# Turning the gated products of a feed-forward network by transposing DMA transfers instead of TensorE

## The chip, the cores and the metric

The kernel runs on one core of a Trainium2 chip. The metric is the device time of one execution in microseconds (us). For the kernel before, three runs gave a median of 916.63 us (916.10 to 916.77). One further execution was recorded by the profiler; it took 917.14 us, of which the profile's span (first to last recorded instruction) is 915.2 us.

## The reference

The reference is an encoder trunk of two layers for one sequence of 256 tokens, 1024 features wide, in float32. A layer mixes tokens by gated linear attention and by grouped attention, then runs a feed-forward network (FFN), then a small gated embedding. The change touches the FFN alone:

```python
FFN_HIDDEN = -(-8 * D_MODEL // (3 * 256)) * 256        # 2816
...
    gate, up = jnp.split(rms_norm(h, g_ffn_pre) @ w_ffn_in, 2, axis=-1)
    h = h + rms_norm((jax.nn.silu(gate) * up) @ w_ffn_out, g_ffn_post)
```

The product `silu(gate) * up` (256 tokens by 2816) is called the gated product below.

## The kernel before, in words

**Numbers.** Every float32 operand of a matrix product is split into a high and a low part, both in the type fp32r: `split` (L131 to L133) casts the high part on ScalarE (ACT) and subtracts it from the source on VectorE (DVE) for the low part. A product then takes three matmul passes (high·high, low·high, high·low) into one PSUM accumulator (`passes`, L113 to L121). TensorE (PE) contracts over partitions, so the left operand of each product has to stand with the contracted index on the partitions.

**Tiles.** Tokens come in two halves `hf` of 128. The 2816 hidden columns are 11 blocks of 256, so a block's gate and up together are 512 columns, one PSUM accumulator `acc`. Blocks 0 and 1 are computed by half: both for half 0, then both for half 1. Blocks 4, 5 and 10 (`PLAIN`) are computed for both halves at once (`block`). The other six blocks come as three pairs (`PAIRS`, beginning at 2, 6 and 8), each by seven products in place of eight in the manner of Strassen (`seven`). "o" steps (`out_step`) multiply finished gated products by `w_ffn_out`. The string `FFN` sets in which order block, pair and "o" steps are written in the program; the products of a block are consumed some 20 us or more after they are made, except those of the last pair.

**The turn.** A gated product comes out with tokens on the partitions (tile `sg`, from the pool `t512`, 128 by 512 float32), and `w_ffn_out` needs it with the hidden index on the partitions. Before the change PE turns it: `transpose_in` (L444 to L452, the transposes at L448) turns n squares of 128 by 128 into a PSUM tile `aux` by multiplying with the identity, and `hid.put` splits that tile into the FFN's `Split` object `hid`, whose tiles come from the pool `big` (ACT casts from PSUM, DVE subtracts from PSUM). `turned` (L1547 to L1552) does so with two squares for each half of blocks 0 and 1 and with four for each half of a pair; `block` has its own `turn` (L1582 to L1592, the transposes at L1587) with four squares for both halves together. In each layer that makes four turns of two squares, three of four squares for the plain blocks, and six of four for the pairs: 44 squares.

**What sets the order.** Each turn is a `Task`: a generator that yields a number of ticks before its next piece is written into the program. A tick comes twice per group of twelve matmuls of 512 columns (2.72 us), so one tick is about 1.36 us. `WAIT_FFN` 4, `WAIT_BLOCK` 6, `WAIT_PAIR` 9 and `WAIT_LAST` (3, 4) are these numbers. The framework's scheduler then makes the final order per engine from its own estimate of durations; `tc.high_priority(AHEAD)` lets the splits of a turn go ahead of other work. On the chip every engine runs its own list strictly in order.

**The weights.** All weights arrive by DMA transfers issued by SyncE (SP) at L296 (class `Stream`) into the pool `raw` (two buffers) or, for the pairs, into buffers lent from other pools (`lent`, `big`). ACT casts them into `wh` tiles and DVE subtracts for `wl` tiles (both L133, four buffers each, 128 by 1024 a half); a `raw` buffer is loaded again when DVE has finished with it. PE uses `wh` and then `wl` of each unit.

The pool `mid` holds tiles of 128 by 1024 float32 (512 KB); `halves` gives the two halves of one.

Of the kernel before, what the change touches and what calls it, by code (L numbers as in the profile page):

```python
# [10 lines left out]
F32 = mybir.dt.float32  # L11
F32R = mybir.dt.float32r
BF16 = mybir.dt.bfloat16
AF = mybir.ActivationFunctionType
ALU = mybir.AluOpType
AX = mybir.AxisListType

P = 128
T = 256
# [4 lines left out]

AHEAD, EMPTY, EMPTY_FIRST = 400, 100, 1600

WAIT, WAIT_FIRST, WAIT_FFN, WAIT_BLOCK = 6, 4, 4, 6

WAIT_NEXT, WAIT_IN, WAIT_H = (7, 9), ((6, 9), (6, 6)), ((3, 5), (3, 5))
WAIT_MIX = 3, 6  # L30
# [11 lines left out]
PLAIN, PAIRS = (4, 5, 10), (2, 6, 8)  # L42
OUT = (0, 1, 2, 3, 4, 5, 10, 6, 7, 8, 9)

WAIT_PAIR, WAIT_LAST = 9, (3, 4)


GATES = "uuu1u2m34m5m67m"
# [11 lines left out]
def trunk_kernel(ctx: ExitStack, tc: tile.TileContext, a: dict, out: bass.AP):  # L60
# [7 lines left out]
    nc = tc.nc  # L68
# [11 lines left out]
    part = ["start"]  # L80
# [8 lines left out]
    def mid(dt=F32):  # L89
        return b4p.tile([P, 1024], dt, tag="mid", name=nm("mid"))  # L90
# [34 lines left out]
    def vmul(out, in0, in1):  # L125
        nc.vector.tensor_tensor(out=out, in0=in0, in1=in1, op=ALU.mult)
# [4 lines left out]
    def split(hi, lo, src):  # L131

        return nc.scalar.copy(hi, src), nc.vector.tensor_tensor(out=lo, in0=src, in1=hi.bitcast(F32), op=ALU.subtract)  # L133
# [310 lines left out]
    def transpose_in(sp, src, k, n, hf, plain=None):  # L444

        ps = aux()
        for i in range(n):
            nc.tensor.transpose(ps[:, i * P : (i + 1) * P], src[:, i * P : (i + 1) * P], ident)  # L448
# [69 lines left out]
    def halves(t):  # L518
        return [t[:, j * 512 : (j + 1) * 512] for j in range(2)]
# [501 lines left out]
    for l in range(DEPTH):  # L1021
# [532 lines left out]
        for hf in range(2):  # L1554
            ws.lend = hf == 1
            for b in range(2):
                o = acc()
                for kh in range(2):
                    amode(o, u2, hf, kh * 4, us[b][kh], kh == 0, kh == 1, fresh=b == 0)
                sg = t512()  # L1560
                nc.scalar.activation(sg[:, 0:256], o[:, 0:256], AF.Silu)
                vmul(sg[:, 0:256], o[:, 256:512], sg[:, 0:256])
                turned(sg[:, 0:256], 2 * b, 2, hf)
                if hf == 1:
                    ws.done(2)
                if (hf, b) == (1, 0):
                    forms = sums(plain)

        def block(b):
            sg = t512()  # L1570
            o = [acc(), acc()]
            for kh in range(2):
                w = ws.take()
                for hf in range(2):
                    amode(o[hf], u2, hf, kh * 4, w, kh == 0, kh == 1)
                if kh == 1:
                    for hf in range(2):
                        c = slice(hf * 256, (hf + 1) * 256)
                        nc.scalar.activation(sg[:, c], o[hf][:, 0:256], AF.Silu)
                        vmul(sg[:, c], o[hf][:, 256:512], sg[:, c])  # L1580

                    def turn():  # L1582
                        yield WAIT_BLOCK
                        ps = aux()
                        for k in range(2):
                            for hf in range(2):
                                nc.tensor.transpose(  # L1587
                                    ps[:, k * T + hf * P : k * T + (hf + 1) * P],
                                    sg[:, hf * 256 + k * P : hf * 256 + (k + 1) * P], ident,
                                )  # L1590
# [3 lines left out]
                    t = Task(turn(), part[0], 2 * b // 4)  # L1594
                    for hf in range(2):
                        hid.makers[hf].append(t)
# [157 lines left out]
```

## Time and profile before

| | |
|---|---|
| median of three runs | 916.63 us |
| profiled execution | 917.14 us |
| span of its profile | 915.2 us |
| granted TensorE clock over the span | 0.999 of full |
| FFN of layer 0 (its turns) | about 266 to 424 us of the span |
| FFN of layer 1 | about 715 to 872 us of the span |

In a row of a profile a group's form `out<-in` names the tiles without their buffer numbers; `acc_0ffnin` is a PSUM accumulator of layer 0's FFN, `wh_0ffnin` and `wl_0ffnin` the parts of its weights. In timelines a row gives the start in us, the length in us, the engine, the line of the kernel, the operation and a count; a bracket at its end gives the idle time before it and who ended that. Rows of a matmul group overlap by a pipeline's depth, so the start of a row to the start of the next is what a group takes. A view of windows gives for each stretch its length and, per engine, the busy time and the count of instructions, then the granted clock, the DMA engines' busy share and GB/s.

### The profile page before, as it was taken

To read this page: it belongs to the slowest core of one execution; us is meant where nothing else is said; L and a number is where in the kernel's file an instruction comes from. 1 tells how busy PE (TensorE), PEld (TensorE's weight loads), DVE (VectorE), ACT (ScalarE), POOL (GpSimd) and SP (SyncE) were. 2 spreads that over 40 slices of the span, in tenths; PEclk is the share of its full clock that TensorE was granted. 3 is DMA by queue.
4 is the path that set the end of the run, shared out by engine and by line. 5 is a ranking of instruction groups with operands and counts; after the bars stand their busy time and mean duration, and the time that the engine had idled before them with its cause. 6 is when DMAs were issued, how large, how long until landed. Compare 5 with 4: busy or idle time off the path is not lost.

```text
span 915.2 us, 12243 instructions
## 1 busy us (share of the span) xinstructions
PE 905.9 (99%) x4551; PEld 769.6 (84%) x4551; DVE 791.1 (86%) x1025; ACT 584.5 (64%) x979; POOL 103.0 (11%) x157
## 2 busy tenths in 40 slices
PE   9999999999999999999999999999999999999996
PEld 8898888888878888888898888888888888888886
DVE  7899989987769998998779899799876898989984
ACT  6688777564567565566675687675644766565563
POOL 3700220400100000000334001110001000000001
PEclk9999999999999999999999999999999999999999
DMA  8664445657485655646576524455573856555361
GB/s 277 218 191 135 139 140 189 214 189 238 143 276 185 210 189 209 222 165 238 179 273 199 170 92 139 138 184 184 197 255 115 279 165 219 212 175 222 134 235 47
DMA packets 89512, 173.45 MB, mean 190 GB/s; under 512 B 3486, under 2 KB 27558, under 8 KB 88940
## 3 DMA queue, kind: packets, MB, share of 16 engines
q1 hardware_dynamic: 89292, 172.53, 55.7%
q8 instruction: 36, 0.59, 0.3%
q14 instruction: 24, 0.20, 0.1%
q10 hardware_dynamic: 160, 0.14, 0.0%
HBM read 169.50 MB, written 3.15 MB: 189 GB/s over the span
## 4 chain that ended last, share of the span: by engine, by line
PE 90%; DVE 4%; DMA 3%; issue 1%; ACT 1%; POOL 0%; SPq 0%; POOLq 0%; ACTq 0%; DVEq 0%
PE acc_1ffnin L121 12%; PE acc_0ffnin L121 10%; PE acc_1gate L121 7%; PE acc_0gate L121 7%; PE acc_1ffnin L105 7%; PE acc_0ffnin L105 4%; PE acc_1rq L121 3%; PE acc_1gqk L105 2%; PE acc_0gqk L105 2%; PE acc_1wout L121 2%; PE acc_0gg L121 2%; PE acc_1gg L121 2%; PE acc_1v L121 2%; PE acc_0v L121 2%; PE acc_1merge L121 2%; PE acc_0merge L121 2%
## 5 line engine op out<-in xcount | busy, mean ns | idle before, releaser
L133 ACT CAST wh_1ffnin<-raw_1ffnin 128x1024 fp32r<-128x1024 f32 x38 | 38.5, 1049 | 26.1 <-DMA raw_1ffnin<-in_w_ffn_out_dram 7.3
L133 ACT CAST wh_0ffnin<-raw_0ffnin 128x1024 fp32r<-128x1024 f32 x38 | 38.4, 1049 | 24.4 <-PE acc_0ffnin L121 7.8
L133 DVE TENSOR_TENSOR wl_1ffnin<-raw_1ffnin,wh_1ffnin 128x1024 fp32r<-128x1024 f32 x38 | 45.0, 1220 | 7.9 <-ACT wh_1ffnin L133 7.7
L133 DVE TENSOR_TENSOR wl_0ffnin<-raw_0ffnin,wh_0ffnin 128x1024 fp32r<-128x1024 f32 x38 | 44.9, 1220 | 7.7 <-ACT wh_0ffnin L133 7.6
L105 PE MATMUL acc_0ffnin<-wh_0ffnin,big_0ffnin 128*128 128x512 f32 x176 | 45.1, 390 | 0.0
L105 PE MATMUL acc_1ffnin<-wh_1ffnin,big_1ffnin 128*128 128x512 f32 x176 | 45.1, 390 | 0.0
L121 PE MATMUL acc_0ffnin<-wh_0ffnin,big_0wout 128*128 128x512 f32 x168 | 42.5, 393 | 0.0
L121 PE MATMUL acc_1ffnin<-wh_1ffnin,big_1wout 128*128 128x512 f32 x168 | 42.5, 393 | 0.0
L105 PEld LDWEIGHTS acc_0ffnin<-wh_0ffnin,big_0ffnin 128*128 128x128 f32 x176 | 33.0, 188 | 6.9
L105 PEld LDWEIGHTS acc_1ffnin<-wh_1ffnin,big_1ffnin 128*128 128x128 f32 x176 | 33.0, 188 | 6.9
L133 DVE TENSOR_TENSOR wl_1ffnin<-lent_1ffnin,wh_1ffnin 128x1024 fp32r<-128x1024 f32 x30 | 35.7, 1216 | 1.7 <-ACT wh_1ffnin L133 1.7
L133 DVE TENSOR_TENSOR wl_0ffnin<-lent_0ffnin,wh_0ffnin 128x1024 fp32r<-128x1024 f32 x30 | 35.7, 1216 | 1.7 <-ACT wh_0ffnin L133 1.7
L121 PEld LDWEIGHTS acc_0ffnin<-wh_0ffnin,big_0wout 128*128 128x128 f32 x168 | 31.1, 188 | 6.2
L121 PEld LDWEIGHTS acc_1ffnin<-wh_1ffnin,big_1wout 128*128 128x128 f32 x168 | 31.1, 188 | 6.2
L133 ACT CAST wh_0ffnin<-lent_0ffnin 128x1024 fp32r<-128x1024 f32 x30 | 30.7, 1053 | 7.1 <-PE acc_0ffnin L105 3.9
L133 ACT CAST wh_1ffnin<-lent_1ffnin 128x1024 fp32r<-128x1024 f32 x30 | 30.7, 1053 | 7.0 <-PE acc_1ffnin L105 3.9
L133 ACT CAST wh_0gate<-raw_0gate 128x1024 fp32r<-128x1024 f32 x20 | 20.0, 1048 | 17.0 <-DMA raw_0gate<-in_w_o_attn_dram 7.8
L133 DVE TENSOR_TENSOR wl_0gate<-raw_0gate,wh_0gate 128x1024 fp32r<-128x1024 f32 x20 | 24.0, 1247 | 7.5 <-ACT wh_0gate L133 7.4
L133 ACT CAST wh_1gate<-raw_1gate 128x1024 fp32r<-128x1024 f32 x20 | 19.9, 1048 | 14.0 <-DMA raw_1gate<-in_w_o_attn_dram 6.1
L133 DVE TENSOR_TENSOR wl_1gate<-raw_1gate,wh_1gate 128x1024 fp32r<-128x1024 f32 x20 | 23.5, 1218 | 5.3 <-ACT wh_1gate L133 5.2
L105 PE MATMUL acc_0ffnin<-wl_0ffnin,big_0ffnin 128*128 128x512 f32 x88 | 24.6, 394 | 0.0
L105 PE MATMUL acc_1ffnin<-wl_1ffnin,big_1ffnin 128*128 128x512 f32 x88 | 24.6, 394 | 0.0
(724 smaller groups left out, 2710.1 us busy)
## 6 DMA issues: line engine op xcount, KB each, us to landing
raw_0ffnin<-in_w_ffn_out_dram SPq DMA_DIRECT2D x11, 1024.0 KB, 5.2
raw_1ffnin<-in_w_ffn_out_dram SPq DMA_DIRECT2D x11, 1024.0 KB, 5.3
lent_0ffnin<-in_w_ffn_in_dram SPq DMA_DIRECT2D x6, 1024.0 KB, 7.3
lent_1ffnin<-in_w_ffn_in_dram SPq DMA_DIRECT2D x6, 1024.0 KB, 7.8
raw_0v<-in_w_in_dram SPq DMA_DIRECT2D x4, 1024.0 KB, 5.1
raw_0gate<-in_w_o_gla_dram SPq DMA_DIRECT2D x4, 1024.0 KB, 5.9
raw_0gate<-in_w_o_attn_dram SPq DMA_DIRECT2D x4, 1024.0 KB, 6.2
raw_0wout<-in_w_ffn_in_dram SPq DMA_DIRECT2D x8, 512.0 KB, 6.2
```

The lines of the kernel that those rows point to most:

```text
L105: return nc.tensor.matmul(o, lhsT, rhs, start=start, stop=stop)
L121: nc.tensor.matmul(o, x, y, start=start and n == 0, stop=stop and n == len(seq) - 1, **kw)
L133: return nc.scalar.copy(hi, src), nc.vector.tensor_tensor(out=lo, in0=src, in1=hi.bitcast(F32), op=ALU.subtract)
```

## The change

Nine of the eleven turns of a layer (all but the two of the last pair, beginning at block 8) no longer use PE. `turn_out` copies the gated product on ACT, read as 16-bit words, into one half of a `mid` tile, all low words of the float32 values first, then all high words ("planes"), and SP issues one DMA that transposes this half (128 by 1024 words, 256 KB, eight squares of 128 by 128) into the other half. Nine ticks later `take_in` joins the planes again on ACT, 16-bit words into float32 values, over the first half, and splits the result into `hid`, from SBUF now. Blocks 0 and 1 of a half share one tile and one turn of four squares, where before they had two turns of two. So a layer loses 36 transposes on PE and gains nine copies that take apart and nine that join, 128 by 1024 16-bit words each, on ACT, and nine transposing transfers on SP's queue; instead of four casts of 256 and nine of 512 columns from PSUM there are nine of 512 from SBUF and two from PSUM, and as many subtractions on DVE. Lines of the changed kernel are those of before plus one up to `transpose_in` and some 28 more behind it.

```diff
-WAIT, WAIT_FIRST, WAIT_FFN, WAIT_BLOCK = 6, 4, 4, 6
+WAIT, WAIT_FIRST = 6, 4
...
-WAIT_PAIR, WAIT_LAST = 9, (3, 4)
+WAIT_TURNED, WAIT_LAST = 9, (3, 4)
...
+    def turn_out(src, k, hf):
+
+        with tc.high_priority(AHEAD):
+            both, turned = halves(mid())
+            turned = turned.bitcast(U16)
+            parts = both.bitcast(U16).rearrange("p (s c) -> p s c", s=2)
+            words = src.bitcast(U16)
+            if hf is None:
+                nc.scalar.copy(
+                    parts.rearrange("p s (k h f) -> p s k h f", k=2, f=P),
+                    words.rearrange("p (h k f s) -> p s k h f", h=2, f=P, s=2),
+                )
+            else:
+                nc.scalar.copy(parts, words.rearrange("p (c s) -> p s c", s=2))
+            nc.sync.dma_start_transpose(out=turned.rearrange("p (x t) -> p x t", t=P), in_=parts.rearrange("p s c -> p (s c)"))
+        return both, turned
+
+    def take_in(sp, both, turned, k, hf):
+
+        n, tn = (2, T) if hf is None else (4, P)
+        hi, lo = sp.at(k, n, (hf or 0) * P, tn)
+        nc.scalar.copy(
+            both.bitcast(U16).rearrange("p (k t s) -> p k t s", s=2, t=tn),
+            turned.rearrange("p (s k t) -> p k t s", s=2, t=tn),
+        )
+        split(hi, lo, both.rearrange("p (k t) -> p k t", t=tn))
...
-        def turned(src, k, n, hf, wait=WAIT_FFN):
-
+        def turned(src, k, hf):

             def turn():
-                yield wait
-                transpose_in(hid, src, k, n, hf)
-
-            hid.makers[hf].append(Task(turn(), part[0], k // 4))
+                if k == 2 * PAIRS[-1]:
+                    yield WAIT_LAST[hf]
+                    transpose_in(hid, src, k, 4, hf)
+                else:
+                    x = turn_out(src, k, hf)
+                    yield WAIT_TURNED
+                    take_in(hid, *x, k, hf)
...
         for hf in range(2):
             ws.lend = hf == 1
+            first = t512()
             for b in range(2):
...
-                sg = t512()
-                nc.scalar.activation(sg[:, 0:256], o[:, 0:256], AF.Silu)
-                vmul(sg[:, 0:256], o[:, 256:512], sg[:, 0:256])
-                turned(sg[:, 0:256], 2 * b, 2, hf)
+                sg = first[:, b * 256 : (b + 1) * 256]
+                nc.scalar.activation(sg, o[:, 0:256], AF.Silu)
+                vmul(sg, o[:, 256:512], sg)
+                if b:
+                    turned(first, 0, hf)
...
-                    def turn():
-                        yield WAIT_BLOCK
-                        ps = aux()
-                        for k in range(2):
-                            for hf in range(2):
-                                nc.tensor.transpose(
-                                    ps[:, k * T + hf * P : k * T + (hf + 1) * P],
-                                    sg[:, hf * 256 + k * P : hf * 256 + (k + 1) * P], ident,
-                                )
-                        with tc.high_priority(AHEAD):
-                            hid.put(ps, 2 * b, 2, 0, T)
...
+                    turned(sg, 2 * b, None)
...
-                turned(sg, 2 * b, 4, hf, WAIT_LAST[hf] if b == PAIRS[-1] else WAIT_PAIR)
+                turned(sg, 2 * b, hf)
```

How this stands in the engines' lists (numbers behind the names are buffers' numbers). PE of the kernel before, at the first turn of a plain block (block 4, layer 0; `big_0wout` and `mid_0ffnin` are parts of the FFN's input):

```order
L121 MATMUL acc_0ffnin_2906<-wl_0ffnin_2854,big_0wout_2470 128x512 x4
L1587 MATMUL aux_0ffnin_2920<-ident,t_0ffnin_2783 128x128 x4
L121 MATMUL acc_0ffnin_2907<-wh_0ffnin_2853,big_0wout_2470 128x512 x8
L121 MATMUL acc_0ffnin_2907<-wl_0ffnin_2854,big_0wout_2470 128x512 x4
L121 MATMUL acc_0ffnin_2864<-wh_0ffnin_2878,mid_0ffnin_2747 128x512 x8
```

In the changed kernel the four transposes are gone, and so is every such group but those of the last pair; the matmul groups around them stand in the same order as before.

ACT of the kernel before, at the turns of blocks 0 and 1 of half 0, layer 0 (L1561 is the `Silu` of these blocks):

```order
L1561 ACTIVATE t_0ffnin_2669<-acc_0ffnin_2622 128x256
L133 CAST big_0ffnin_2666<-aux_0ffnin_2663 128x2x128
L1561 ACTIVATE t_0ffnin_2702<-acc_0ffnin_2672 128x256
L133 CAST big_0ffnin_2666<-aux_0ffnin_2697 128x2x128
L133 CAST wh_0ffnin_2711<-raw_0wout_2522 128x1024 x2
L133 CAST mid_0ffnin_2738<-mid_0wout_2297 128x512
```

The same place of the changed kernel (L468 takes apart, L476 joins):

```order
L1596 ACTIVATE t_0ffnin_2594<-acc_0ffnin_2622 128x256
L453 COPY mid_0wout_2298<-aux_0wout_2643 128x512
L468 COPY mid_0ffnin_2665<-t_0ffnin_2594 128x1024
L476 COPY mid_0ffnin_2665<-mid_0ffnin_2665 128x1024
L1596 ACTIVATE t_0ffnin_2668<-acc_0ffnin_2669 128x256
L134 CAST wh_0ffnin_2702<-raw_0wout_2522 128x1024 x2
L134 CAST mid_0ffnin_2729<-mid_0wout_2297 128x512
```

The first join stands directly behind the copy that feeds its transfer, so ACT waits there for the whole transfer, with a weight cast behind it. At the second turn two casts of 512 columns and a unit of weights stand between the two copies; in layer 1 the first turn's join stands nine rows further down, behind the second turn's take-apart.

SP's list at that place in the changed kernel; before, it held the same loads with none of the transposing transfers between them:

```order
L297 DMA raw_0emb_2589<-in_w_ffn_in_dram 128x4x256 x2
L469 DMA_TRANSPOSE mid_0ffnin_2665<-mid_0ffnin_2665 128x8x128
L297 DMA lent_0ffnin_2696<-in_w_ffn_in_dram 128x4x512
L297 DMA lent_0ffnin_2700<-in_w_ffn_in_dram 128x4x512
L297 DMA raw_0ffnin_2708<-in_w_ffn_in_dram 128x4x256 x2
L297 DMA raw_0ffnin_2761<-in_w_ffn_in_dram 128x4x256
L469 DMA_TRANSPOSE mid_0ffnin_2752<-mid_0ffnin_2752 128x8x128
L297 DMA raw_0ffnin_2761<-in_w_ffn_in_dram 128x4x256
L469 DMA_TRANSPOSE mid_0ffnin_2840<-mid_0ffnin_2840 128x8x128
```

Each transposing transfer waits on SP for its take-apart copy, with weight loads behind it; the load of `big_0ffnin` (one megabyte) that stood behind `raw_0emb` before now stands two units earlier.

More of the change, by code (lines that the diff above doesn't have):

```diff
@@ L13 @@
 BF16 = mybir.dt.bfloat16
+U16 = mybir.dt.uint16
 AF = mybir.ActivationFunctionType
@@ L1543, in trunk_kernel @@
         us = [[ws.take() for _ in range(2)] for _ in range(2)]
-        def turned(src, k, n, hf, wait=WAIT_FFN):
+        def turned(src, k, hf):
             def turn():
-                yield wait
-                transpose_in(hid, src, k, n, hf)
-            hid.makers[hf].append(Task(turn(), part[0], k // 4))
+                if k == 2 * PAIRS[-1]:
[5 more added lines that the diff above has]
+                    take_in(hid, *x, k, hf)
+            t = Task(turn(), part[0], k // 4)
+            for i in range(2) if hf is None else (hf,):
+                hid.makers[i].append(t)
         for hf in range(2):
             ws.lend = hf == 1
+            first = t512()
             for b in range(2):
@@ L1580, in block @@
                         vmul(sg[:, c], o[hf][:, 256:512], sg[:, c])
-                    def turn():
-                        yield WAIT_BLOCK
-                        ps = aux()
-                        for k in range(2):
-                            for hf in range(2):
-                                nc.tensor.transpose(
-                                    ps[:, k * T + hf * P : k * T + (hf + 1) * P],
-                                    sg[:, hf * 256 + k * P : hf * 256 + (k + 1) * P], ident,
-                                )
-                        with tc.high_priority(AHEAD):
-                            hid.put(ps, 2 * b, 2, 0, T)
-                    t = Task(turn(), part[0], 2 * b // 4)
-                    for hf in range(2):
-                        hid.makers[hf].append(t)
+                    turned(sg, 2 * b, None)
                 ws.done()
```

## The prediction

> **What bounds the kernel now.** I read the profile's totals and its chain first, then who waits for what on PE, then the stretches of the FFN. The totals and the first row of the chain:
>
> ```profile
> PE 905.9 (99%) x4551; PEld 769.6 (84%) x4551; DVE 791.1 (86%) x1025; ACT 584.5 (64%) x979; POOL 103.0 (11%) x157
> PE 90%; DVE 4%; DMA 3%; issue 1%; ACT 1%; POOL 0%; SPq 0%; POOLq 0%; ACTq 0%; DVEq 0%
> ```
>
> PE is busy 905.9 of 915.2 us and makes 90% of the chain. All that it waits for, over the whole span:
>
> ```profile
> PE warm L105 <- POOL seed L142: 1.0, 1, 1.0
> PE aux_1emb L994 <- DMA mid_0ffnout<-in_p_dram: 0.6, 1, 0.6
> PE acc_0rq L105 <- ACT wh_start L142: 0.5, 1, 0.5
> PE acc_0ffnin L121 <- ACT wh_0emb L133: 0.2, 1, 0.2
> ```
>
> Only the last wait, 0.2 us, lies in an FFN. So work taken off PE there is time won, until a weight tile comes too late. The view of windows: the two FFNs, then the densest 20 us of layer 0:
>
> ```profile
> 265.00:425.00 160.00, 160.00 (x727) 131.94 (x726) 146.88 (x145) 99.63 (x126) 0.95 (x1) 1.00 0.58 201
> 715.00:872.00 157.00, 157.00 (x717) 129.98 (x717) 143.63 (x143) 95.62 (x122) 0.00 (x0) 1.00 0.59 205
> 285.00:305.00 20.00, 20.00 (x92) 16.55 (x91) 20.00 (x19) 12.66 (x17) 0.00 (x0) 1.00 0.36 129
> ```
>
> PE has no gap. DVE (third pair of numbers) is busy 146.88 of 160 us and all of the 20; ACT (fourth) has 60 us free. The DMA engines are 0.58 busy.
>
> **The transposes that go.** The rows of the PSUM tile that they write:
>
> ```profile
> L448 PE MATMUL aux_0ffnin<-ident,t_0ffnin x32: 270/272/329, 266.8 to 421.7; 128*128 128x128 f32 x32
> L133 ACT CAST big_0ffnin<-aux_0ffnin x13: 360/579/588, 270.2 to 422.0; 128x512 fp32r<-128x512 f32 x9, 128x256 fp32r<-128x256 f32 x4
> L133 DVE TENSOR_TENSOR big_0ffnin<-aux_0ffnin,big_0ffnin x13: 414/680/692, 271.4 to 422.6; 128x512 fp32r<-128x512 f32 x9, 128x256 fp32r<-128x256 f32 x4
> L1587 PE MATMUL aux_0ffnin<-ident,t_0ffnin x12: 270/272/273, 297.9 to 340.9; 128*128 128x128 f32 x12
> ```
>
> Of 32 + 12 squares a layer, eight stay (the last pair): 36 go, in four bursts of two and seven of four. Their 272 ns overlap their neighbours, so I price a burst by the starts of rows in PE's timeline:
>
> ```profile
> 272.61 0.38 PE L448 MATMUL aux_0ffnin<-ident,t_0ffnin 128*128 128x128 f32 x2
> 272.75 2.08 PE L121 MATMUL acc_0ffnin<-wh_0wout,big_0wout 128*128 128x512 f32 x8
> 274.66 1.07 PE L121 MATMUL acc_0ffnin<-wl_0wout,big_0wout 128*128 128x512 f32 x4
> ...
> 297.88 0.60 PE L1587 MATMUL aux_0ffnin<-ident,t_0ffnin 128*128 128x128 f32 x4
> 298.24 2.08 PE L121 MATMUL acc_0ffnin<-wh_0ffnin,big_0wout 128*128 128x512 f32 x8
> 300.16 1.07 PE L121 MATMUL acc_0ffnin<-wl_0ffnin,big_0wout 128*128 128x512 f32 x4
> 301.07 1.98 PE L121 MATMUL acc_0ffnin<-wh_0ffnin,mid_0ffnin 128*128 128x512 f32 x8
> 302.88 1.07 PE L121 MATMUL acc_0ffnin<-wl_0ffnin,mid_0ffnin 128*128 128x512 f32 x4
> ```
>
> Eight matmuls alone take 302.88 − 301.07 = 1.81 us. With a burst of four ahead they take 300.16 − 297.88 = 2.28, so the burst costs 0.47; with two, 274.66 − 272.61 = 2.05, so 0.24. A layer gives back 7 × 0.47 + 4 × 0.24 = 4.25 us, both layers **8.5 us**. This is the whole gain; all else is cost, hidden or not.
>
> **Work added on ACT and DVE.** No 16-bit copy is in the trace. The nearest rows by count of elements, then by bytes:
>
> ```profile
> L133 ACT CAST wh_0ffnin<-raw_0ffnin 128x1024 fp32r<-128x1024 f32 x38 | 38.4, 1049 | 24.4 <-PE acc_0ffnin L121 7.8
> 275.24 1.67 ACT L133 CAST mid_0ffnin<-mid_0wout 128x512 fp32r<-128x512 f32 x3
> ```
>
> So a copy of 1024 words lies between about 0.55 us (as many bytes) and 2.1 us (twice the first row, if a stride of two words doubled it); I take 1.05, the row with as many elements. Eighteen copies a layer add 18.9 us to ACT's 99.6 of 160, less than its 60 us free; at 2.1 they would add 37.8, still less, but with no room in dense places. Casts and subtractions of the splits are a wash: on DVE 4 × 0.41 + 9 × 0.68 = 7.8 us before, 9 × 0.63 from SBUF (the rate of such subtractions in DVE's timeline) + 2 × 0.68 = 7.0 after. ACT also loses its waits for PE's transposes. None of this is on PE, so I cost it at nothing; the cover is the lead that weights have on PE, below.
>
> **The new wait.** ACT now waits at each join for a transfer, with weight casts queued behind it, DVE's subtractions waiting for those, and PE for both. Two numbers decide: T, from SP's issue to landing, and what ACT may be late.
>
> T is not in the trace. Rows of DMA issues (KB each, median us to landing):
>
> ```profile
> out_dram<-h SPq DMA_DIRECT2D x3, 256.0 KB, 2.0
> mid_0ffnout<-in_p_dram SPq DMA_DIRECT2D x1, 256.0 KB, 6.2
> lent_0ffnin<-in_w_ffn_in_dram SPq DMA_DIRECT2D x6, 1024.0 KB, 7.3
> mid_0ffnin<-in_g_ffn_post_dram SPq DMA_DIRECT2D x1, 512.0 KB, 8.3
> ```
>
> A plain transfer of the same 256 KB takes 2.0 us at the kernel's end with nothing ahead and 6.2 with traffic; 8.3 is the longest row. So T lies in 2.0 to 8.3, and above if turning is slower than copying. I take 4, midway between the two rows of the same size, since the DMA engines are 0.58 busy.
>
> Lateness is read from weights that follow a turn. The first turn of layer 0 is the worst: its join stands directly behind its take-apart. Rows of PE (what the product waits for, and the use of the weights behind it), ACT and DVE:
>
> ```profile
> 265.73 1.16 PE L121 MATMUL acc_0ffnin<-wl_0emb,big_0wout 128*128 128x512 f32 x4
> ...
> 273.34 2.01 ACT L133 CAST wh_0ffnin<-raw_0wout 128x1024 fp32r<-128x1024 f32 x2
> ...
> 274.50 2.35 DVE L133 TENSOR_TENSOR wl_0ffnin<-raw_0wout,wh_0ffnin 128x1024 fp32r<-128x1024 f32 x2
> ...
> 292.05 2.35 DVE L133 TENSOR_TENSOR wl_0ffnin<-raw_0ffnin,wh_0ffnin 128x1024 fp32r<-128x1024 f32 x2
> ...
> 280.37 1.08 PE L121 MATMUL acc_0ffnin<-wl_0ffnin,big_0wout 128*128 128x512 f32 x4
> ...
> 296.98 1.07 PE L121 MATMUL acc_0ffnin<-wl_0ffnin,big_0wout 128*128 128x512 f32 x4
> ```
>
> The product ends at 266.9; Silu 0.4, multiply 0.4 and take-apart 1.05 end at 268.8. The transfer lands at 268.8 + T, the join (1.05) and the next Silu (0.4) follow, and the weight cast that began at 273.34 begins at 270.2 + T: late by T − 3.1, 0.9 us at T = 4. Its low part was ready at 276.85 and used at 280.37, a lead of 3.5; but DVE then works without a gap to 305, and its tightest lead is at 294.4 against 296.98, 2.6 us. Four bursts less let PE come 1.0 earlier, which leaves 1.6. The first join therefore costs T − 4.7, nothing at 4.
>
> For the other joins the work between take-apart and join on ACT covers T: in layer 0 about 3.1, 3.3, 2.0, 6.6, 6, long, 4.6 and 3 us (of the order's rows at the durations above), in layer 1 the same but for the first (long) and second (4.2). With the next lead, 3.5, such a join costs T − gap − 3.5, nothing at T = 4. I allow **1 us** in all for meetings of several of them.
>
> **SP's queue.** Each transposing transfer waits on SP for ACT's take-apart, with weight loads behind it. SP waits anyway:
>
> ```profile
> SPq L296 <- DVE wl_0ffnin L133: 107.1, 21, 11.1
> ```
>
> 107 us in this FFN and its edges are spent waiting for DVE to free buffers, so a few tenths per issue vanish there; if an issue took several us, it would appear with T. The nine transfers of 256 KB move 2.4 MB a layer through engines 0.58 busy: hidden. One load of 1 MB now goes ahead of a unit that PE met 0.2 us late, and a store of 1 MB goes behind it. The first falls into idle DMA time; I cost the pair at 0, between −0.2 and +1.
>
> Sum against the profiled execution: 917.14 − 8.5 + 1 = 909.6; it ran 0.5 above the median of 916.63, so **909.1 us** on that scale.
>
> **A page against the change.** The Trainium skill, page "VectorE: DVE Perf Modes", section "The three transpose paths", lists 1309 ns for a 128×128 bf16 square by the DMA crossbar against 390 ns on TensorE, and its rules prefer TensorE where PSUM will do. If eight squares followed one another at that price, an estimate from that page gives T = 10.5, and the formulas for the stalls then give some 45 us, a time of about 953. The Trainium skill, "DMA: Bandwidth & Descriptors", section "Latency and other measured facts", gives transposing DMAs 261 GB/s, by which 256 KB move in 1.0 us, an estimate, and T stays near the short row. No row here shows either; PE's own square costs 0.12 us by the rows above.
>
> **Rivals.**
>
> Forecast, T up to 6: stalls of at most 1.3 for the first join and 0.5 each for the two with 2.0 us of cover, 2.3 in all. 908.1 to 911.5.
>
> Slower: **transposing is slow, so ACT stalls at its joins** with weights behind. Stalls by the formulas: at T = 7, 2.3 for the first, 2 × 1.5 where the cover is 2.0 us, 0.4 + 2 × 0.2 where it is 3.1 and 3.3, 2 × 0.5 where it is 3, together 7.1; at T = 7.2 they reach 8.5, where the change begins to lose; at T = 8.3, the longest row, 3.6 + 2 × 2.8 + 1.7 + 2 × 1.5 + 2 × 1.8 + 2 × 0.2 + 0.6 = 18.5, so 917.1 − 8.5 + 18.5 − 0.5 = 926.6, this rival's time. For it: nothing in the trace turns by DMA, the first join has no cover, DVE is at 92%. Against: the 2.0 us row. This is also the rival to which the page's price leads.
>
> No change: T near 7, or **DVE becomes the bound**: where it is busy 20 of 20 us, PE's pull-ahead finds weights late, and its 13.1 us of slack in this FFN shrink to 8.9 when the FFN is 4.25 shorter. For it: the lead of 2.6. Against: the gain by that place is 1.0, less than the lead. About 914.8 to 918.4.
>
> In between: ACT's copies cost 2.1 and eat part of the leads, 912 to 914.8.
>
> **How the numbers follow.** Forecast 0.45, in between 0.13, no change 0.08, slower 0.34. About 0.2% (1.8 us) is what a measurement of this kernel can tell from no change. Faster by more than that: 0.45 + 0.13 = 0.58; within it 0.08; slower 0.34. Faster's own range is 907.5 (no stall, the 0.2 gone, half a us of scatter) to 914.8. To leave out at most 2 in 10, the range must reach into the slow rival, over its time at the longest row: 907.5 to 930; what is left out is mostly T beyond 8.5.
>
> **What would show it.** Right: no row of PE with `ident` in the FFN but for the last pair; PE's busy time some 8 us less; the transfers landing in about 4 us; PE's waits still near 2 us. Wrong: PE waiting for `wl_0ffnin` or `wh_0ffnin` shortly behind a join, ACT's waits on the transposing transfer over 3 us each, ACT copies over 1.5 us, or DVE without a gap in the whole FFN. If the first turn of layer 0 stalls and that of layer 1 does not, T lies between 5 and 7.

## The result and the profile after

The changed kernel took 911.17 us (median of six runs, 909.68 to 911.95) beside 915.79 us for the kernel before (median of six in all). The ratio is 0.9947 with a 95% interval of 0.9934 to 0.9959: faster by 0.53%, 4.9 us. Run again later, beside experiments, it came to 0.9934 (0.9921 to 0.9948), 6.1 us. The profiled execution took 909.68 us, with a span of 907.9.

The totals and the chain, from the page of the kernel after:

```profile
PE 898.8 (99%) x4479; PEld 762.2 (84%) x4479; DVE 790.2 (87%) x1021; ACT 620.5 (68%) x1011; POOL 105.9 (12%) x157
PE 78%; DVE 11%; DMA 4%; issue 4%; ACT 2%; POOL 0%; SPq 0%; POOLq 0%; ACTq 0%; DVEq 0%
```

PE has 72 instructions and 7.1 us less, ACT 36 us more. PE's share of the chain fell from 90% to 78%, and DVE's rose from 4% to 11%: somewhere PE now runs at the pace of its weights. PE's waits over the whole span look harmless:

```profile
PE warm L106 <- POOL seed L143: 1.0, 1, 1.0
PE acc_0ffnin L106 <- DVE wl_0ffnin L134: 0.6, 2, 0.3
PE acc_0ffnin L122 <- DVE wl_0ffnin L134: 0.2, 1, 0.2
PE aux_0ffnout L449 <- DVE h L611: 0.2, 1, 0.2
```

All three waits for `wl` lie in layer 0, and PE waits 2.0 us in all. The windows of the two FFNs show the new load: ACT 115.51 and 116.82 us where it had 99.63 and 95.62, DVE about as busy as before (146.45 where it had 146.88, 146.66 where it had 143.63), and the DMA engines' share up from 0.58 and 0.59 to 0.70.

```profile
265.00:425.00 160.00, 159.10 (x699) 129.55 (x698) 146.45 (x143) 115.51 (x141) 1.41 (x3) 1.00 0.70 219
715.00:872.00 157.00, 157.00 (x698) 130.04 (x697) 146.66 (x145) 116.82 (x143) 0.86 (x2) 1.00 0.70 217
```

Where the time came from is best read off marks that both kernels have: the first matmul of each layer's FFN and one of the last. The view by tile gives first and last start of a group. Before:

```profile
L121 PE MATMUL acc_0ffnin<-wh_0wout,big_0wout x48: 389/389/478, 254.3 to 274.4; 128*128 128x512 f32 x48
L121 PE MATMUL acc_1ffnin<-wh_1wout,big_1wout x64: 387/389/481, 706.6 to 728.7; 128*128 128x512 f32 x64
L105 PE MATMUL acc_1ffnin<-wh_1ffnin,big_1ffnin x176: 387/389/481, 783.0 to 884.9; 128*128 128x512 f32 x176
```

After:

```profile
L122 PE MATMUL acc_0ffnin<-wh_0wout,big_0wout x48: 389/389/476, 253.7 to 273.1; 128*128 128x512 f32 x48
L122 PE MATMUL acc_1ffnin<-wh_1wout,big_1wout x64: 387/389/477, 703.6 to 725.3; 128*128 128x512 f32 x64
L106 PE MATMUL acc_1ffnin<-wh_1ffnin,big_1ffnin x176: 387/389/474, 778.2 to 877.7; 128*128 128x512 f32 x176
```

Layer 1's FFN went from 884.9 − 706.6 = 178.3 us to 877.7 − 703.6 = 174.1: **4.2 us won**, the 4.25 of the prediction. From the first mark of layer 0 to that of layer 1 the gain is (706.6 − 254.3) − (703.6 − 253.7) = **2.4 us**: 1.8 less. (The 0.6 us before the first mark is ahead of anything that the change touches. Layer 0's stretch also holds a wait of 0.6 us for `in_p` that the kernel before had, so it can win up to some 4.9.)

The loss sits where the prediction looked for it, behind the first join of layer 0. ACT's timeline there (the bracket is the idle time before a row and what ended it):

```profile
267.19 1.05 ACT L468 COPY mid_0ffnin<-t_0ffnin 128x1024 uint16<-128x1024 uint16 x1
274.00 1.17 ACT L476 COPY mid_0ffnin<-mid_0ffnin 128x1024 uint16<-128x1024 uint16 x1 [5.76 <-DMA mid_0ffnin<-mid_0ffnin]
275.07 0.38 ACT L1596 ACTIVATE t_0ffnin<-acc_0ffnin 128x256 f32<-128x256 f32 x1
275.35 1.99 ACT L134 CAST wh_0ffnin<-raw_0wout 128x1024 fp32r<-128x1024 f32 x2
```

ACT stands for 5.76 us, and the weight cast that began at 273.34 begins at 275.35, two us late by the clock and 2.6 by PE, whose first mark stands 0.6 us earlier: the prediction's T − 3.1 at T = 5.7. DVE hands the lateness on, since it works without a gap behind it, down to the unit that had the lead of 2.6 us:

```profile
293.92 2.35 DVE L134 TENSOR_TENSOR wl_0ffnin<-raw_0ffnin,wh_0ffnin 128x1024 fp32r<-128x1024 f32 x2
```

It ends at 296.27, and PE is there first:

```profile
293.33 2.30 PE L122 MATMUL acc_0ffnin<-wh_0ffnin,big_0wout 128*128 128x512 f32 x8
295.46 0.62 PE L122 MATMUL acc_0ffnin<-wl_0ffnin,big_0wout 128*128 128x512 f32 x2
296.33 0.74 PE L122 MATMUL acc_0ffnin<-wl_0ffnin,big_0wout 128*128 128x512 f32 x2 [0.24 <-DVE wl_0ffnin L134]
296.91 2.02 PE L122 MATMUL acc_0ffnin<-wh_0ffnin,big_0wout 128*128 128x512 f32 x8
...
341.39 0.63 PE L106 MATMUL acc_0ffnin<-wl_0ffnin,big_0ffnin 128*128 128x512 f32 x2
342.36 0.73 PE L106 MATMUL acc_0ffnin<-wl_0ffnin,big_0ffnin 128*128 128x512 f32 x2 [0.35 <-DVE wl_0ffnin L134]
342.93 2.00 PE L106 MATMUL acc_0ffnin<-wh_0ffnin,big_0ffnin 128*128 128x512 f32 x8
```

From start to start, the eight matmuls at 293.33 take 2.13 us instead of 1.81, and the four behind them 1.45 instead of 0.91: 0.9 us lost, of which the view of waits names 0.24. The rest of a stall is in longer steps between rows, so the marks are the better measure. The same happens at 341.39, 1.54 instead of 0.91, where three turns are packed into ACT's list: 0.6 more.

A stretch that holds both stalls and neither end of the FFN begins with the group at 274.66 in the kernel before (shown in the prediction) and ends with this one:

```profile
387.29 1.09 PE L121 MATMUL acc_0ffnin<-wl_0ffnin,big_0wout 128*128 128x512 f32 x4
```

The same two groups in the kernel after, and the third wait for `wl`, which lies outside:

```profile
273.38 1.07 PE L122 MATMUL acc_0ffnin<-wl_0wout,big_0wout 128*128 128x512 f32 x4
383.75 1.07 PE L122 MATMUL acc_0ffnin<-wl_0ffnin,big_0wout 128*128 128x512 f32 x4
420.48 0.73 PE L106 MATMUL acc_0ffnin<-wl_0ffnin,big_0ffnin 128*128 128x512 f32 x2 [0.25 <-DVE wl_0ffnin L134]
```

The stretch takes 112.63 us before and 110.37 after, 2.3 won; the experiments below show 3.8 where nothing is late, so some 1.6 are lost here. Around the third wait, at the end of layer 0's FFN, from the group that began at 420.43 before and 417.08 after to the turn of `h` (428.61 and 426.41), PE needs 9.33 us instead of 8.18, 1.15 more. The kernel without any turn, below, loses 0.6 there, so the transfers are at most a part of that cause; the rest is open. The wait for `in_p` that goes gives 0.8 back.

The tile that is turned shows what transfers and copies cost (min, median and max in ns, then first and last start):

```profile
L469 SPq DMA_TRANSPOSE mid_0ffnin<-mid_0ffnin x9: 1237/1250/1922, 268.3 to 377.1; - x9
L476 ACT COPY mid_0ffnin<-mid_0ffnin x9: 1168/1177/1183, 274.0 to 380.8; 128x1024 uint16<-128x1024 uint16 x9
L468 ACT COPY mid_0ffnin<-t_0ffnin x6: 1038/1044/1047, 267.2 to 376.0; 128x1024 uint16<-128x1024 uint16 x6
```

The copies take 1.04 and 1.18 us. The list of DMA issues gives a landing of 3.3 us in layer 0 and 3.6 in layer 1. These are not medians of nine: the profile tells the landing of one transfer in layer 0 and of three in layer 1.

```profile
mid_0ffnin<-mid_0ffnin SPq DMA_TRANSPOSE x9, 3.3
mid_1ffnin<-mid_1ffnin SPq DMA_TRANSPOSE x9, 3.6
```

The first of layer 0 is far off, issued at 268.3 and landed at 274.0: 5.7 us. ACT's waits at its joins tell of more: the second of layer 0, issued at 283.93, lets ACT go on at 290.24, 6.3 us later, of which ACT stands 3.4; the third and fourth take 3.2 and 3.6. The second does not hold DVE up: it works without a gap from 275.48 past 296.

### The profile page after: what moved, and what is told of

Read it like the earlier page. It is cut to its first block, busy times and chain, and to the rows that moved or that the text cites. A ratio compares the mean times of both kernels' runs of the same rounds, so it can differ in the third digit from the quotient of the medians.

```text
span 907.9 us, 12157 instructions
## 1 busy us (share of the span) xinstructions
PE 898.8 (99%) x4479; PEld 762.2 (84%) x4479; DVE 790.2 (87%) x1021; ACT 620.5 (68%) x1011; POOL 105.9 (12%) x157
## 4 chain that ended last, share of the span: by engine, by line
PE 78%; DVE 11%; DMA 4%; issue 4%; ACT 2%; POOL 0%; SPq 0%; POOLq 0%; ACTq 0%; DVEq 0%
PE acc_1ffnin L122 12%; PE acc_0gate L122 7%; PE acc_1gate L122 7%; PE acc_1ffnin L106 7%; DVE wl_0ffnin L134 6%; PE acc_1rq L122 3%; PE acc_0gqk L106 2%; PE acc_1gqk L106 2%; PE acc_1wout L122 2%; PE acc_0ple L122 2%; PE acc_1v L122 2%; PE acc_0gg L122 2%; PE acc_1gg L122 2%; PE acc_0v L122 2%; PE acc_0merge L122 2%
```

## The experiments

The theory after the result: all 8.5 us are there, and what is missing is lost in layer 0, because the first join has no cover and its transfer takes long. Rivals: ACT's added copies, the load of the transposing transfers on the DMA engines, and the packed stretch of ACT later in layer 0.

**No turn at all.** The split takes the product as it stands.

```diff
-                    x = turn_out(src, k, hf)
                     yield WAIT_TURNED
-                    take_in(hid, *x, k, hf)
+                    n, tn = (2, T) if hf is None else (4, P)
+                    split(*hid.at(k, n, (hf or 0) * P, tn), src.rearrange("p (k t) -> p k t", t=tn))
```

> Nine ticks after a gated product is done it is split as it stands, untransposed: no take-apart copy, no transfer, no join, so what w_ffn_out multiplies is left unturned. It keeps what the change removes (36 squares a layer on PE) and drops all that it adds. If PE's bursts are worth 8.5 us and nothing else limits the FFN (both theories), the time is 8 to 8.5 us under before: 0.9905 to 0.9915 of it. If the FFN of layer 0 is held by its weights even then (the rival that DVE or the weight loads are the bound), it gains only 5 to 7 us: 0.9925 to 0.9945.

Measured: 0.9915 (0.9901 to 0.9928), 7.8 us under before, at the edge of the 8 to 8.5 expected, and by the marks 4.1 us in layer 0 and 4.2 in layer 1, which is below called what a layer keeps. The PE term of the prediction holds within the interval. At the end of layer 0's FFN (before: 420.43 to 428.61) PE loses 0.6 us here too. This is about what any way of turning off PE can reach.

**Copies without transfers.**

```diff
-            parts = both.bitcast(U16).rearrange("p (s c) -> p s c", s=2)
+            parts = turned.rearrange("p (s c) -> p s c", s=2)
...
-            nc.sync.dma_start_transpose(out=turned.rearrange("p (x t) -> p x t", t=P), in_=parts.rearrange("p s c -> p (s c)"))
```

> The take-apart copy writes where the transfer would have written, and the join reads it there: both ACT copies stay, the transposing transfer is left out (so the squares are not turned). Theory of the wait (ACT stands at the joins until the transfer lands, and weights come late): nothing waits, so 7.5 to 8.5 us under before, like the kernel without any turn. Rival, ACT's 18 copies a layer themselves make weights late: stays at the changed kernel's 4.9 us under before, 0.994 to 0.996.

Measured: 0.9921 (0.9909 to 0.9933), 7.2 us under before, a little short of the 7.5 expected; layer 0 keeps 4.4 us. The copies are all but hidden: the rival that the copies alone keep the time at 4.9 us under before falls.

**A plain transfer in the transposing one's place.**

```diff
-            nc.sync.dma_start_transpose(out=turned.rearrange("p (x t) -> p x t", t=P), in_=parts.rearrange("p s c -> p (s c)"))
+            nc.sync.dma_start(turned, parts.rearrange("p s c -> p (s c)"))
```

> The same program order as the changed kernel, but each transfer of 256 KB copies its half tile plainly instead of transposing it (the squares are not turned). Theory of the wait: a plain transfer lands in 2.5 to 4 us in place of 3.3 to 6.2, ACT's first wait in layer 0 falls from 5.8 to under 4 us, and 7 to 8 us are gained against before. Rival that the place in the queue behind a megabyte of weights sets the wait, not the turning: the first wait stays above 5 us, and the gain near 5.

Measured: 0.9937 (0.9925 to 0.9949). The expectation of the theory failed in its first half. The first join of this kernel on ACT:

```profile
275.05 1.17 ACT L476 COPY mid_0ffnin<-mid_0ffnin 128x1024 uint16<-128x1024 uint16 x1 [6.69 <-DMA mid_0ffnin<-mid_0ffnin]
```

A plain copy of 256 KB at this place lands no sooner, 6.6 us after its issue at 268.4, and layer 0 keeps only 0.9 us while layer 1 keeps 4.2. So the rival came out: at this place the wait costs, whether the transfer turns or not. What sets the wait is taken up with the store below.

**Transfers that nobody waits for.**

```diff
-                    x = turn_out(src, k, hf)
+                    turn_out(src, k, hf)
                     yield WAIT_TURNED
-                    take_in(hid, *x, k, hf)
+                    n, tn = (2, T) if hf is None else (4, P)
+                    split(*hid.at(k, n, (hf or 0) * P, tn), src.rearrange("p (k t) -> p k t", t=tn))
```

> Take-apart copies and transposing transfers as in the changed kernel, but nothing reads what they bring: the split takes the unturned product, without a join. So the transfers' load on SP's queue and the DMA engines stays and ACT's wait and join go. Theory of the wait: 7.5 to 8.5 us under before. Rival, transposing transfers take the DMA engines from the weights (the engines' share in the FFN rose from 0.58 to 0.70): 4 to 6 us under before, with more waits of ACT on weights' transfers than without.

Measured: 0.9932 (0.9919 to 0.9945), between the two expectations. The marks decide more sharply than the time: layer 0 keeps 4.2 us and layer 1 4.2, although the DMA engines are as loaded as in the changed kernel:

```profile
265.00:425.00 160.00, 159.68 (x706) 130.93 (x705) 148.61 (x146) 107.39 (x134) 1.83 (x3) 1.00 0.72 221
```

In this profile the load alone delays PE's weights no more than in the kernel without any turn: PE waits 0.2 us for `wl` in both. The time leaves open up to 1.5 us for it, taken as the distance from the kernel without any turn, which is within the two intervals.

**The changed kernel again.** No edit.

> The changed kernel itself once more, for a second profile and more runs beside the others. Theory (layer 1 gives its whole 4.25 us, layer 0 loses about 2 of them at the first join and where its lateness shows later): 0.994 to 0.996 of before again, the stall in layer 0 again and none in layer 1.

Measured: 0.9934 (0.9921 to 0.9948). The stall was not there again in its profile:

```profile
272.98 1.17 ACT L476 COPY mid_0ffnin<-mid_0ffnin 128x1024 uint16<-128x1024 uint16 x1 [3.94 <-DMA mid_0ffnin<-mid_0ffnin]
```

Same program, same place: this time the first transfer landed 3.9 us after its issue (269.07), and layer 0 kept 3.9 us, layer 1 4.2. This execution took 908.60 us where the one with 5.7 us took 909.68. The others of this kernel lie between 909.09 and 911.95; what the first transfer took in them, no profile shows.

**The first join later.** It is held on ACT behind the last Silu of blocks 0 and 1.

```diff
+        silu = [None]
...
-                nc.scalar.activation(sg, o[:, 0:256], AF.Silu)
+                silu[0] = nc.scalar.activation(sg, o[:, 0:256], AF.Silu)
...
                     yield WAIT_TURNED
-                    take_in(hid, *x, k, hf)
+                    with tc.issue_after(silu[0].ins) if l == 0 and k == 0 and hf == 0 else nullcontext():
+                        take_in(hid, *x, k, hf)
```

> One join is moved: that of the first turn of layer 0 is held on ACT behind the Silu of block 1, half 1, which puts it behind the second turn's take-apart, as layer 1 has it. Transfers, copies and all else stay. Theory of the wait at this one join: ACT's wait of 5.8 us there goes, layer 0 keeps some 4 us, and the time falls by 1 to 2.5 us to 0.992 to 0.9935. Rival, the loss in layer 0 comes from the transfers' load or from ACT's packed stretch later (about 320 to 350 us): no change from the changed kernel, 0.9945 to 0.996.

Measured: 0.9927 (0.9915 to 0.9940). Layer 0 keeps 4.7 us, as the theory has it, but layer 1 only 2.9 in this profile, whose chain runs through two loads of weights there; why they were late is open. Its ratio is 0.0007 below that of the changed kernel on the same chip, its median 0.2 us above: the time does not tell them apart.

**The first turn back on PE.**

```diff
-                if k == 2 * PAIRS[-1]:
-                    yield WAIT_LAST[hf]
+                if k == 2 * PAIRS[-1] or l == k == hf == 0:
+                    yield WAIT_LAST[hf] if k else 4
                     transpose_in(hid, src, k, 4, hf)
```

> One turn is undone: the first of layer 0 (blocks 0 and 1, half 0) goes back to four transposes on PE after four ticks; the other 17 stay as changed. It gives back 0.47 us of PE. Theory of the first join: the stall that it caused, 1 to 2.5 us, goes, so 0.5 to 2 us faster than the changed kernel, 0.9925 to 0.9942. Rival (load, packed ACT): 0.2 to 0.5 us slower than the changed kernel.

Measured: 0.9919 (0.9907 to 0.9932), 908.41 us, 0.9 us under the changed kernel's median on the same chip though it pays one burst on PE. PE waits for no weights in its FFNs; layer 0 keeps 5.0 us, layer 1 only 3.3, its chain running through the same two loads. The direction is the theory's, the size within the scatter.

**Issued by ACT.**

```diff
-            nc.sync.dma_start_transpose(
+            nc.scalar.dma_start_transpose(
```

> The transposing transfers are issued by ACT behind its take-apart, on ACT's own DMA queue, not behind the weights' loads on SP's. If the first transfer takes 5.7 us because a megabyte of weights is ahead of it in SP's queue (the plain one took 6.6 there), it lands in 3 to 4 us here and layer 0's stall shrinks; against that, 18 issues of 1.25 us now stand on ACT, 11 us a layer: together within 1.5 us of the changed kernel either way. If the engines are simply shared between queues, the first transfer stays at 5 us or more and the time rises by 1 to 3 us.

Measured: 1.0454 (1.0435 to 1.0473), 41 us slower than before. Neither expectation came near. ACT at the first join, then ACT's waits at the joins of both layers, and what PE waits for most:

```profile
279.95 1.16 ACT L476 COPY mid_0ffnin<-mid_0ffnin 128x1024 uint16<-128x1024 uint16 x1 [10.79 <-DMA mid_0ffnin<-mid_0ffnin]
```

```profile
ACT mid_0ffnin L476 <- DMA mid_0ffnin<-mid_0ffnin: 34.4, 6, 10.8
ACT mid_1ffnin L476 <- DMA mid_1ffnin<-mid_1ffnin: 17.7, 6, 7.7
```

```profile
PE acc_0ffnin L122 <- ACT wh_0ffnin L134: 11.9, 4, 4.3
PE acc_1ffnin L122 <- ACT wh_1ffnin L134: 5.3, 3, 3.7
```

On a queue of its own the first transfer takes 10.7 us, and SP no longer holds the two loads of 1 MB behind it: they are issued at 269.07, it at 269.19. This is the prediction's slow rival in the flesh. By its formula the first join costs T − 4.7 = 6.0 us. The issues themselves, 18 of 1.25 us, add 22 us of work to ACT, so not all of the 41 are waits.

**The store behind the first transfer.** On SP, one store of 1 MB changes places. `turns` collects the issues of the transposing transfers.

```diff
         if l == 0:
-            kept = keep_embedding()
+            made = next(embedding)
+            kept = keptp.tile([P, 2, D], F32, tag="kept", name=nm("kept"))
...
+        if l == 0:
+            with tc.issue_after(turns[0].ins):
+                nc.sync.dma_start(kept, made)
```

> The changed kernel with one transfer moved on SP's queue: the store of 1 MB (the embedding kept for later) that was issued at about 260.5 us, eight us ahead of the first transposing transfer, now follows that transfer and two loads. ACT's order stays as in the changed kernel, the first join directly behind its take-apart. If the first transfer's 3.9 to 5.7 us come from the backlog of the DMA engines (busy all of 264 to 276 us), it now lands in 3 to 3.6 us, ACT's first wait falls under 3.5 us, layer 0 keeps 4 us and the time is 0.9915 to 0.993 of before. Rival, the time is the transposing itself or the loads behind it: 3.9 to 5.7 us as before and 0.9934 to 0.9947.

Measured: 0.9923 (0.9909 to 0.9938), 908.63 us. ACT at the first join:

```profile
271.84 1.17 ACT L478 COPY mid_0ffnin<-mid_0ffnin 128x1024 uint16<-128x1024 uint16 x1 [3.63 <-DMA mid_0ffnin<-mid_0ffnin]
```

The transfer lands 3.6 us after its issue (268.24), and layer 0 keeps 4.9 us, layer 1 4.2, with the join still directly behind its take-apart. That fits the backlog; but one of the changed kernel's own profiles had 3.9, and the interval overlaps with 0.9934, so this one profile alone would not settle the cause of T.

The DMA packets in the traces go further. The two loads of 512 KB issued 2.7 us ahead of the first transposing transfer move in packets of 1 KB, the store in packets of 8 KB, the transfer in packets of 256 bytes. In all six profiles in which SP issues that transfer, its last packet ends 0.91 us after the last packet of these two loads. The loads end 2.1 and 2.3 us after the transfer's issue in the two kernels with the store moved; where the store is ahead, 2.4 us in the profile with 3.9, and 3.9 to 4.9 in three others (4.1 in the one with 5.7). The store's own last packet lies 1.2 us before the issue in the profile with 3.9, and 0.3 to 0.7 in the three. So the first transfer waits for the loads ahead of it, and these are late where the store still ran among them. That is six profiles, not a time of many runs.

**Plain transfers issued by ACT.** `nc.scalar.dma_start(turned, ...)` in the transposing transfer's place.

> Plain transfers of the same 256 KB in place of the transposing ones (the squares are not turned), issued by ACT on its own queue, as in the kernel whose transposing transfers took 4.4 to 10.7 us there. If a second queue shares the engines packet by packet with the weights' loads, and the 256-byte packets of the transposing transfer lose by that, the plain one with its 2 KB packets lands in 3 to 6 us and the time is 0.99 to 1.00 of before. If any transfer on a second queue is late whatever its packets, it lands in 7 us or more and the time stays above 1.03.

Measured: 1.0174 (1.0147 to 1.0200), between the two expectations. The lists of DMA issues give the plain transfer's median landing, first on SP's queue (the kernel above), then on ACT's (this one):

```profile
mid_0ffnin<-mid_0ffnin SPq DMA_DIRECT2D x9, 256.0 KB, 4.3
mid_1ffnin<-mid_1ffnin SPq DMA_DIRECT2D x9, 256.0 KB, 3.0
```

```profile
mid_0ffnin<-mid_0ffnin ACTq DMA_DIRECT2D x9, 256.0 KB, 5.6
mid_1ffnin<-mid_1ffnin ACTq DMA_DIRECT2D x9, 256.0 KB, 4.4
```

So on the second queue the transfers land later, by 1.3 and 1.4 us, though these rows rest on few landings (one and three on SP's queue, one and five on ACT's), and the kernel is 22 us slower than with the plain transfer on SP's (18 issues of 0.47 us on ACT included); that it transposes costs 26 more (issues of 1.25 us included). How the engines share out their time between queues, these runs do not show.

**Store and first join both later.** The moves of the first join and of the store, together. The edit is the sum of the two above.

> All nine turns a layer by transposing transfers, the store moved behind the first of them, and the first join of layer 0 held behind the second turn's take-apart. With no wait left that outlasts its cover, it keeps what a kernel without any turn keeps, less the copies' part: 0.9915 to 0.9925 of before. If the later packed stretch of ACT in layer 0 or the joins of layer 1 still cost, 0.993 to 0.9945.

Measured: 0.9924 (0.9911 to 0.9937), 908.55 us; layer 0 keeps 4.6 us, layer 1 4.2. It adds nothing to the store's move alone. Three orders (0.9919, 0.9923, 0.9924) are below both measurements of the changed kernel by their medians and come within 0.8 us of the kernel without any turn; against the changed kernel of 0.9947 and 0.9934 the intervals overlap in part.

What a layer keeps carries a scatter: ahead of 274.66, where no more than one burst of 0.24 us is gone, the kernels already differ by 1.1 us. The stretch between two groups of layer 0 (274.66 to 387.29 in the kernel before) tells the kernels apart where the whole time does not. In us:

| kernel | loads ahead end, after the transfer's issue | ACT's wait at the first join | won in the stretch |
|---|---|---|---|
| changed, first profile | 4.1 | 5.8 | 2.3 |
| changed, again | 2.4 | 3.9 | 3.8 |
| plain transfer | 5.4 | 6.7 | 0.5 |
| traffic only | 3.9 | no join | 3.8 |
| first join later | 4.9 | 0 | 3.8 |
| store later | 2.1 | 3.6 | 3.8 |
| store and join later | 2.3 | 0 | 3.8 |
| first turn on PE | no transfer | no join | 3.8 |
| copies without transfers | no transfer | 0 | 3.7 |
| no turn at all | no transfer | no join | 3.8 |

With the first join later, the transfer is as late as ever and nothing is lost. So it is ACT's wait at this one join that costs. The packed stretch of ACT at 320 to 350 us stands in the kernels with 3.8 too; by itself it loses nothing, and costs only where DVE is already late.

## Why the prediction was right, and where its size was off

It forecast 909.1 us, 7.5 under the median it had, with a range to 930; measured were 4.9 and, again, 6.1 us. The mechanism, the sign and the place of the loss were right.

- **The transposes** (8.5 us): right. Layer 1 gave 4.2 or 4.3 in both profiles of the changed kernel and in six others. In layer 0 the stretch of the table gave 3.7 or 3.8 wherever the first wait was short or gone. At the FFN's end 0.6 to 1.0 us are lost in all of these but the kernel with the first turn on PE, the kernel without any turn included, and 0.8 is won at `in_p`.
- **ACT's copies** (1.05 us each, hidden): right. 1.04 and 1.18 us; the kernel with copies and no transfers is within 0.6 us of the one with neither.
- **DVE as the bound**: not by itself. It is busy 146.45 of 160 us in layer 0, as before, and PE passes with a wait of 0.2 to 0.3 us when ACT is on time, as it does without any turn. But once ACT is late, DVE has no gap in which to catch up.
- **T of 4 us**: the term that was mis-sized, at the first two joins of layer 0. Elsewhere 3.1 to 4.3 us can be read in the two profiles of the changed kernel, near the 4 taken, which was luck as much as reasoning: the two rows it stood between were of other places and other loads. The first transfer, with no cover, took 5.7 us in one profile and 3.9 in another, and 4.7 is where it begins to cost. The second took 6.3, which by the formula (T less a cover of 3.1 and a lead of 3.5) costs nothing. The formula T − 4.7 for the first gives 1.0 us at 5.7; PE lost 0.9 there, and nothing at 3.9. What I took from the midpoint of two rows should have been worked out from what SP had issued just before at this very place: 3 MB within the nine us ahead of it (SP's timeline: two loads of 512 KB at 259.4, the store at 260.4, two loads at 265.5).
- **The allowance of 1 us**: too small. Behind a late first join DVE stays late, and at ACT's packed stretch, 320 to 350 us, PE lost another 0.6; the prediction had no term for a lateness that comes back. In the first profile layer 0 loses 1.8 us net; in the medians 2.4 to 3.6 of the 8.5 are missing, by the two ratios, of which the kernel without any turn misses 0.7. The rest is not shown by any profile, since the profiled executions were the fastest of their runs.
- **The slow rival** (T over 7.2): not this kernel. Its sign, a wait of ACT over 3 us, did appear at two joins (5.8 and 3.4 us), and the sign for T between 5 and 7, a stall in layer 0 and none in layer 1, fits the first profile. Transfers on ACT's queue made the rival real, 41 us.
- **The load that moved ahead and the store that moved behind** (priced at 0): the load was harmless; PE's wait for the first weights, 0.2 us before, is gone in one profile of the changed kernel and 0.2 in the other. The store then stood eight us ahead of the first transposing transfer and still ran among the loads that this transfer waited for; behind it, the loads ended at 2.1 and 2.3 us, against 2.4 and 4.1 in the changed kernel's two profiles.

## What to carry to other kernels

Work taken off the engine that bounds a stage is won as far as the detour's copies are hidden, its waits covered, and the next weights still in time; check each wait separately, in every place where the schedule puts it, since the one with no cover, out of eighteen, ate a fifth of this gain in the first profile. Where an in-order engine waits for a transfer, price the transfer by the queue that it meets at that moment, not by a median elsewhere in the trace. Before giving such transfers a queue of their own, see what the shared queue holds back for them.

## What the runs showed of the hardware

- A transposing transfer of 256 KB within SBUF, eight squares of 128 by 128 16-bit words, landed in 3.9 to 6.3 us at the first two joins of layer 0 and in 3.1 to 4.3 elsewhere, as far as its landing can be read. A plain one took 6.6 at the first of them. What is ahead on the queue tells: in all six profiles the first transfer's last packet ended 0.91 us after the last packet of the loads ahead. The Trainium skill ("VectorE: DVE Perf Modes", "The three transpose paths") lists 1309 ns per 128×128 square by the crossbar; eight one after another would be 10.5 us, an estimate from that page, and the traces show less than half of it elsewhere than at the first two joins.
- It keeps the DMA engines busier than a plain one. Packets of the page after, then of the page before:

```profile
DMA packets 108519, 178.16 MB, mean 196 GB/s; under 512 B 22494, under 2 KB 46566, under 8 KB 107948
```

```profile
DMA packets 89512, 173.45 MB, mean 190 GB/s; under 512 B 3486, under 2 KB 27558, under 8 KB 88940
```

  19,007 packets more for 18 transfers are 1056 each, all under 512 bytes. In layer 0's FFN the engines' busy share rose by 0.12 of 160 us, over nine transfers 2.1 us of all sixteen engines for each; against the kernel without any turn (0.59) it is 2.0. This is an upper bound: in the two us that hold most of the first transfer (270 to 272) the view gives a share of 1.64, more than all sixteen have, so the time that it counts for these packets holds waiting too. With plain transfers the share rose by 0.04, 0.7 us each (0.5 against 0.59), in the row of that kernel:

```profile
265.00:425.00 160.00, 157.70 (x690) 127.65 (x689) 144.75 (x141) 114.40 (x139) 0.95 (x1) 1.00 0.62 215
```

- Its issue holds SP for 1.25 us (median in layer 0), the plain one's for 0.47.
- 16-bit copies on ACT with a stride of two words on one side took 1.04 and 1.18 us for 1024 elements in each partition, about as long as a float32 cast of as many (1.05); no other size was run.
- The Trainium skill ("DMA: Bandwidth & Descriptors", "Rules for kernel authors") says that spreading DMAs over the issuing engines does not help, as they share the same sixteen DMA engines. The runs agree and go further: here it cost 22 us with plain transfers and 46 to 48 with transposing ones, the issues on ACT included.
- In layer 0's FFN of the kernel with transposing issues on ACT, PE is busy 145.30 of 160 us and its granted clock is 0.96 (third number from the end); with plain issues on ACT it is busy 152.08, and the clock 1.00. At what length of gaps the clock falls, these runs do not show.

```profile
265.00:425.00 160.00, 145.30 (x599) 115.00 (x600) 125.94 (x121) 102.68 (x125) 0.95 (x1) 0.96 0.64 183
```
